# Row-wise cosine similarity: two rows per partition in three shared slots, products in place, all loads on the Sync queue

## Chip, cores and metric

One core of one Trainium2 chip (trn2). The metric is the device time of one execution in microseconds, the median of several runs. All times below are in microseconds unless ns is written.

## What is computed

```python
x, y: float32 [8192, 8192]
x_norm = np.linalg.norm(x, axis=1, keepdims=True)
y_norm = np.linalg.norm(y, axis=1, keepdims=True)
out = np.sum(x * y, axis=1) / (x_norm.squeeze() * y_norm.squeeze() + 1e-8)
```

For each of 8192 rows three sums over 8192 columns are needed: x·x, y·y and x·y. Each input is 268 MB and is read once; the output is 32 KB.

## The kernel before, in words

The 8192 rows are cut into 64 tiles of 128 rows, one row of 32 KB per partition. `xpool` and `ypool` have two buffers each, so two tiles of x and two of y fit. `issue_dma(t)` loads x of tile t from the Sync queue (SP, L63) and y of tile t from ScalarE's queue (ACT, L64), 4 MB each. The last tile is loaded in pieces: x in two halves (L59), y in pieces of 2048, 2048, 2048, 1024 and 1024 columns (L61).

`compute_tile(t)` gives VectorE (DVE) one fused multiply-and-sum over the tile (L96, which reads x and y, writes the products as bf16 into `prod_s` that nobody reads, and puts the sum into a column of `xy_acc`) and ScalarE two squares with sums (L106 for x, L112 for y, with `sq_s` as unread output). After each tile the load of tile t + 2 into the same buffers is issued, when both engines are done with them.

When tile 61 has been given out, `chain` turns the sums of tiles 0 to 61 into results: a product `nn` on DVE (L120), a square root `den` on ACT (L124), a reciprocal and a product on DVE, a transpose on TensorE, a copy and a store. The rest, after tile 62, is the last tile, piece by piece: squares on ACT (L167, L173 for x; L180 for y), a first piece of x squared on DVE (L157), products on DVE (L186), folds of the pieces' sums (L196, L200, L204), and the same chain for the last two tiles (L208 to L223).

The order on each engine is set by a scheduler from the program's order; a buffer of a pool is handed to the next tile when its last user is done. On DVE `nn` (L120) stands behind the product of tile 62; on ACT `den` (L124) stands ahead of the square of x of tile 62.

Of the kernel before, what the change touches and what calls it, by code (L numbers as in the profile page):

```python
# [7 lines left out]


@with_exitstack  # L10
def kernel(
# [5 lines left out]
):  # L17
    nc = tc.nc
    P = nc.NUM_PARTITIONS

    n_rows, n_cols = x.shape
    assert n_rows % P == 0
    n_tiles = n_rows // P

    fp32 = mybir.dt.float32
    bf16 = mybir.dt.bfloat16

    xv = x.rearrange("(t p) k -> t p k", p=P)
    yv = y.rearrange("(t p) k -> t p k", p=P)

    xpool = ctx.enter_context(tc.tile_pool(name="xpool", bufs=2))
    ypool = ctx.enter_context(tc.tile_pool(name="ypool", bufs=2))
    sqpool = ctx.enter_context(tc.tile_pool(name="sqpool", bufs=1))
    prodpool = ctx.enter_context(tc.tile_pool(name="prodpool", bufs=1))
    accpool = ctx.enter_context(tc.tile_pool(name="accpool", bufs=1))
    finpool = ctx.enter_context(tc.tile_pool(name="finpool", bufs=1))
    psumpool = ctx.enter_context(tc.tile_pool(name="psum", bufs=1, space=bass.MemoryType.PSUM))

    xtiles = [
        xpool.tile([P, n_cols], fp32, tag="x", name=f"xt{t}")  # L40
        for t in range(n_tiles)
    ]
    ytiles = [
        ypool.tile([P, n_cols], fp32, tag="y", name=f"yt{t}")
        for t in range(n_tiles)
    ]

    last = n_tiles - 1

    HALF = n_cols // 2  # L50

    XCH = [(0, HALF), (HALF, n_cols)]
    Q = n_cols // 8
    YCH = [(0, 2 * Q), (2 * Q, 4 * Q), (4 * Q, 6 * Q), (6 * Q, 7 * Q), (7 * Q, n_cols)]

    def issue_dma(t):
        if t == last:
            for a, b in XCH:
                nc.sync.dma_start(out=xtiles[t][:, a:b], in_=xv[t, :, a:b])  # L59
            for a, b in YCH:  # L60
                nc.scalar.dma_start(out=ytiles[t][:, a:b], in_=yv[t, :, a:b])  # L61
        else:
            nc.sync.dma_start(out=xtiles[t], in_=xv[t])  # L63
            nc.scalar.dma_start(out=ytiles[t], in_=yv[t])  # L64

    issue_dma(0)
    issue_dma(1)

    dummy = finpool.tile([P, 1], fp32, tag="dummy")
    nc.scalar.memzero(dummy)  # L70
    nc.scalar.sqrt(out=dummy, in_=dummy)  # L71

    ident = finpool.tile([P, P], fp32, tag="ident")
    make_identity(nc, ident)

    xx_acc = accpool.tile([P, n_tiles], fp32, tag="xx")
    yy_acc = accpool.tile([P, n_tiles], fp32, tag="yy")
    xy_acc = accpool.tile([P, n_tiles], fp32, tag="xy")

    prod_s = prodpool.tile([P, n_cols], bf16, tag="prod")  # L80
    sq_s = sqpool.tile([P, n_cols], bf16, tag="sq")

    res = finpool.tile([P, n_tiles], fp32, tag="res")
    nn = finpool.tile([P, n_tiles], fp32, tag="nn")
    den = finpool.tile([P, n_tiles], fp32, tag="den")
    rcp = finpool.tile([P, n_tiles], fp32, tag="rcp")
    res_t_ps = psumpool.tile([n_tiles, P], fp32, tag="res_t_ps")
    res_t = finpool.tile([n_tiles, P], fp32, tag="res_t")
    res_t_ps_last = psumpool.tile([2, P], fp32, tag="res_t_ps_last")
    res_row_last = finpool.tile([2, P], fp32, tag="res_row_last")  # L90
    out_v = out.rearrange("(t p) -> t p", p=P)

    def compute_tile(t):
        xt = xtiles[t]
        yt = ytiles[t]
        nc.vector.tensor_tensor_reduce(  # L96
            out=prod_s,
            in0=xt,
            in1=yt,
            scale=1.0,  # L100
            scalar=0.0,
            op0=mybir.AluOpType.mult,
            op1=mybir.AluOpType.add,
            accum_out=xy_acc[:, t:t + 1],
        )
        nc.scalar.activation(  # L106
            out=sq_s,
            in_=xt,
            func=mybir.ActivationFunctionType.Square,
            accum_out=xx_acc[:, t:t + 1],  # L110
        )
        nc.scalar.activation(  # L112
            out=sq_s,
            in_=yt,
            func=mybir.ActivationFunctionType.Square,
            accum_out=yy_acc[:, t:t + 1],
        )

    def chain(cols, ps, sb, orows):
        nc.vector.tensor_tensor(  # L120
            out=nn[:, cols], in0=xx_acc[:, cols], in1=yy_acc[:, cols],
            op=mybir.AluOpType.mult,
        )
        nc.scalar.activation(  # L124
            out=den[:, cols], in_=nn[:, cols],
            func=mybir.ActivationFunctionType.Sqrt,
        )
        nc.vector.reciprocal(out=rcp[:, cols], in_=den[:, cols])  # L128
        nc.vector.tensor_tensor(  # L129
            out=res[:, cols], in0=xy_acc[:, cols], in1=rcp[:, cols],  # L130
            op=mybir.AluOpType.mult,
        )
        nc.tensor.transpose(out=ps, in_=res[:, cols], identity=ident)  # L133
        nc.vector.tensor_copy(out=sb, in_=ps)
        nc.sync.dma_start(out=out_v[orows, :], in_=sb)

    for t in range(n_tiles - 1):
        compute_tile(t)
        if t + 2 < n_tiles:
            issue_dma(t + 2)  # L140
        if t == n_tiles - 3:
            e = slice(0, last - 1)
            chain(e, res_t_ps[e, :], res_t[e, :], e)

    lcol = slice(last, last + 1)
    tcols = slice(last - 1, last + 1)
    xt = xtiles[last]
    yt = ytiles[last]
    SPL = 2048
    xxp = accpool.tile([P, 3], fp32, tag="xxp")  # L150
    nych = len(YCH)
    yyp = accpool.tile([P, nych], fp32, tag="yyp")
    xyp = accpool.tile([P, nych], fp32, tag="xyp")
    xx_fold_s = accpool.tile([P, 3], fp32, tag="xxfolds")
    yy_fold_s = accpool.tile([P, nych], fp32, tag="yyfolds")

    nc.vector.tensor_tensor_reduce(  # L157
        out=prod_s[:, 0:SPL],
        in0=xt[:, 0:SPL],
        in1=xt[:, 0:SPL],  # L160
        scale=1.0,
        scalar=0.0,
        op0=mybir.AluOpType.mult,
        op1=mybir.AluOpType.add,
        accum_out=xxp[:, 0:1],
    )
    nc.scalar.activation(  # L167
        out=sq_s[:, SPL:HALF],
        in_=xt[:, SPL:HALF],
        func=mybir.ActivationFunctionType.Square,  # L170
        accum_out=xxp[:, 1:2],
    )
    nc.scalar.activation(  # L173
        out=sq_s[:, HALF:],
        in_=xt[:, HALF:],
        func=mybir.ActivationFunctionType.Square,
        accum_out=xxp[:, 2:3],
    )
    for k, (a, b) in enumerate(YCH):
        nc.scalar.activation(  # L180
            out=sq_s[:, a:b],
            in_=yt[:, a:b],
            func=mybir.ActivationFunctionType.Square,
            accum_out=yyp[:, k:k + 1],
        )
        nc.vector.tensor_tensor_reduce(  # L186
            out=prod_s[:, a:b],
            in0=xt[:, a:b],
            in1=yt[:, a:b],
            scale=1.0,  # L190
            scalar=0.0,
            op0=mybir.AluOpType.mult,
            op1=mybir.AluOpType.add,
            accum_out=xyp[:, k:k + 1],
        )
    nc.scalar.activation(  # L196
        out=xx_fold_s, in_=xxp, func=mybir.ActivationFunctionType.Copy,
        accum_out=xx_acc[:, lcol],
    )
    nc.scalar.activation(  # L200
        out=yy_fold_s, in_=yyp, func=mybir.ActivationFunctionType.Copy,
        accum_out=yy_acc[:, lcol],
    )
    nc.vector.tensor_reduce(  # L204
        out=xy_acc[:, lcol], in_=xyp, axis=mybir.AxisListType.X,
        op=mybir.AluOpType.add,
    )
    nc.vector.tensor_tensor(  # L208
        out=nn[:, tcols], in0=xx_acc[:, tcols], in1=yy_acc[:, tcols],
        op=mybir.AluOpType.mult,  # L210
    )
    nc.scalar.activation(  # L212
        out=den[:, tcols], in_=nn[:, tcols],
        func=mybir.ActivationFunctionType.Sqrt,
    )
    nc.vector.reciprocal(out=rcp[:, tcols], in_=den[:, tcols])
    nc.vector.tensor_tensor(  # L217
        out=res[:, tcols], in0=xy_acc[:, tcols], in1=rcp[:, tcols],
        op=mybir.AluOpType.mult,
    )  # L220
    nc.tensor.transpose(out=res_t_ps_last[0:2, :], in_=res[:, tcols], identity=ident)  # L221
    nc.vector.tensor_copy(out=res_row_last[0:2, :], in_=res_t_ps_last[0:2, :])  # L222
    nc.sync.dma_start(out=out_v[last - 1:last + 1, :], in_=res_row_last[0:2, :])  # L223


# [1 line left out]
_INS = ['x', 'y']  # L227
_OUTS = [((8192,), 'float32')]
# [25 lines left out]
```

## Time and profile before

| | us |
|---|---|
| median of 3 runs (lowest, highest) | 1271.8 (1271.54, 1272.02) |
| the profiled execution | 1271.54 |
| its span, first to last instruction | 1269.8 |
| busy: DVE / ACT | 561.2 / 914.4 |
| L96 product, 128x8192, one | 8.693 |
| L106 and L112 square, 128x8192, one | 7.030 |
| L186 product, 128x2048 / 128x1024 | 2.292 / 1.189 |
| L180 square, 128x2048 / 128x1024 | 1.892 / 1.038 |
| load of 4 MB, issue to landing, median: x (Sync) / y (ACT) | 29.6 / 24.9 |
| DMA packets of 32768 B | 16128 of 19227 |

The DMA share is the mean busy share of the core's 16 DMA engines; a load of 128 partitions is spread over all 16, eight partitions to each. "Landing" is the time at which the last of the 16 has reported. An engine's idle time is put down to what released it.

### The profile page before, as it was taken

What the parts mean: (1) busy time and instruction counts of PE and PEld (TensorE: products, weight loads), DVE (VectorE), ACT (ScalarE), POOL (GpSimd) and SP (SyncE); (2) the same over time, 40 slices, a digit from 0 to 9 for tenths busy, and PEclk for the clock granted to TensorE, in tenths of its full rate; (3) what the DMA queues carried; (4) which work ended last, traced back from release to release, by engine and by line L of the source; (5) the groups of instructions that cost most, each with busy time, mean ns of one, the idle gap of its engine ahead of it and who ended that gap; (6) DMA issues with size and microseconds to landing.
All of it is one profiled execution on the core that took longest, in us unless ns stands there. A gap on an engine that the chain in (4) does not pass through costs nothing.

```text
span 1269.8 us, 874 instructions
## 1 busy us (share of the span) xinstructions
PE 0.8 (0%) x2; PEld 0.2 (0%) x2; DVE 561.2 (44%) x147; ACT 914.4 (72%) x276; POOL 0.7 (0%) x6
## 2 busy tenths in 40 slices
PE   0000000000000000000000000000000000000000
PEld 0000000000000000000000000000000000000000
DVE  2354354453453543534534435445345354353454
ACT  3786686776776867767768668677686686776748
POOL 0000000000000000000000000000000000000000
DMA  9999999999999999999999999999999999999992
GB/s 412 430 429 429 429 433 434 437 430 430 429 429 433 434 433 434 430 429 429 434 434 431 434 431 429 429 435 433 431 431 433 429 431 435 430 433 431 433 424 110
DMA packets 19227, 536.97 MB, mean 423 GB/s; under 512 B 2132, under 2 KB 2196, under 8 KB 2452
## 3 DMA queue, kind: packets, MB, share of 16 engines
q10 hardware_dynamic: 9792, 268.44, 49.2%
q1 hardware_dynamic: 9428, 268.47, 49.2%
q14 instruction: 7, 0.06, 0.0%
HBM read 536.87 MB, written 0.03 MB: 423 GB/s over the span
## 4 chain that ended last, share of the span: by engine, by line
DMA 68%; issue 15%; DVE 11%; ACT 5%; DVEq 0%; PE 0%; SPq 0%
DMA xt<-in_x_dram 36%; DMA yt<-in_y_dram 32%; DVE prod_s L96 11%; ACT sq_s L112 3%; ACT sq_s L106 2%; ACT sq_s L180 1%; ACT L71 0%; DVEq L96 0%; PE res_t_ps_last L221 0%; DVE xy_acc L96 0%; SPq L63 0%; DVE res_row_last L222 0%; ACT sq_s L173 0%; ACT sq_s L167 0%; ACT den L212 0%
## 5 line engine op out<-in xcount | busy, mean ns | idle before, releaser
L96 DVE CUSTOM_DVE_ANT_0 prod_s<-xt,yt 128x8192 bf16<-128x8192 f32 x63 | 547.6, 8693 | 689.7 <-DMA yt<-in_y_dram 656.2
L106 ACT ACTIVATE sq_s<-xt 128x8192 bf16<-128x8192 f32 x63 | 442.9, 7030 | 334.0 <-DMA xt<-in_x_dram 334.0
L112 ACT ACTIVATE sq_s<-yt 128x8192 bf16<-128x8192 f32 x63 | 442.9, 7030 | 1.9
L106 ACT ACTIVATION_READ_ACCUMULATOR sq_s<-xt 128x1 f32 x63 | 11.8, 187 | 0.0
L112 ACT ACTIVATION_READ_ACCUMULATOR sq_s<-yt 128x1 f32 x63 | 11.7, 186 | 0.0
L124 ACT ACTIVATE den<-nn 128x62 f32<-128x62 f32 x1 | 0.3, 255 | 14.3 <-DVE nn L120 14.3
L186 DVE CUSTOM_DVE_ANT_0 prod_s<-xt,yt 128x2048 bf16<-128x2048 f32 (+1 forms) x5 | 9.3, 1851 | 2.1 <-DMA yt<-in_y_dram 2.0
L180 ACT ACTIVATE sq_s<-yt 128x2048 bf16<-128x2048 f32 (+1 forms) x5 | 7.8, 1551 | 0.0
L208 DVE TENSOR_TENSOR nn<-xx_acc,yy_acc 128x2 f32<-128x2 f32 x1 | 0.2, 162 | 14.0 <-ACT yy_fold_s L200 14.0
L96 DVE DVE_READ_ACCUMULATOR2_ANT xy_acc<- 128x1 f32 x63 | 5.2, 83 | 0.0
L173 ACT ACTIVATE sq_s<-xt 128x4096 bf16<-128x4096 f32 x1 | 3.6, 3599 | 0.0
L70 ACT ACT_TABLE_LOAD x1 | 1.3, 1283 | 1.6 <-PEq L238 1.6
L157 DVE CUSTOM_DVE_ANT_0 prod_s<-xt 128x2048 bf16<-128x2048 f32 x1 | 2.3, 2286 | 0.0
L167 ACT ACTIVATE sq_s<-xt 128x2048 bf16<-128x2048 f32 x1 | 1.9, 1909 | 0.0
L71 ACT ACT_TABLE_LOAD x1 | 1.3, 1283 | 0.0
L133 PE MATMUL res_t_ps<-ident,res 128*62 128x128 f32 x1 | 0.4, 393 | 1251.0 <-DVE res L129 1251.0
L180 ACT ACTIVATION_READ_ACCUMULATOR sq_s<-yt 128x1 f32 x5 | 0.9, 186 | 0.0
L128 DVE RECIPROCAL rcp<-den 128x62 f32<-128x62 f32 x1 | 0.5, 535 | 0.0
L222 DVE COPY res_row_last<-res_t_ps_last 2x128 f32<-2x128 f32 x1 | 0.3, 279 | 0.5 <-PE res_t_ps_last L221 0.5
L186 DVE DVE_READ_ACCUMULATOR2_ANT xyp<- 128x1 f32 x5 | 0.4, 82 | 0.0
L221 PE MATMUL res_t_ps_last<-ident,res 128*2 128x128 f32 x1 | 0.4, 373 | 15.7 <-DVE res L217 15.7
L212 ACT ACTIVATE den<-nn 128x2 f32<-128x2 f32 x1 | 0.2, 203 | 0.2 <-DVE nn L208 0.2
(23 smaller groups left out, 3.9 us busy)
## 6 DMA issues: line engine op xcount, KB each, us to landing
yt<-in_y_dram ACTq DMA_DIRECT2D x63, 4096.0 KB, 24.9
xt<-in_x_dram SPq DMA_DIRECT2D x63, 4096.0 KB, 29.6
xt<-in_x_dram SPq DMA_DIRECT2D x2, 2048.0 KB, 25.4
yt<-in_y_dram ACTq DMA_DIRECT2D x3, 1024.0 KB, 20.4
yt<-in_y_dram ACTq DMA_DIRECT2D x2, 512.0 KB, 21.7
out_dram<-res_t SPq DMA_DIRECT2D x1, 31.0 KB
out_dram<-res_row_last SPq DMA_DIRECT2D x1, 1.0 KB
```

Source lines behind the costliest of these rows:

```text
L70: nc.scalar.memzero(dummy)
L71: nc.scalar.sqrt(out=dummy, in_=dummy)
L96: nc.vector.tensor_tensor_reduce(out=prod_s, in0=xt, in1=yt, scale=1.0, scalar=0.0, op0=mybir.AluOpType.mult, op1=mybir.AluOpType.add, acc ...
L106: nc.scalar.activation(out=sq_s, in_=xt, func=mybir.ActivationFunctionType.Square, accum_out=xx_acc[:, t:t + 1],)
L112: nc.scalar.activation(out=sq_s, in_=yt, func=mybir.ActivationFunctionType.Square, accum_out=yy_acc[:, t:t + 1],)
L128: nc.vector.reciprocal(out=rcp[:, cols], in_=den[:, cols])
L133: nc.tensor.transpose(out=ps, in_=res[:, cols], identity=ident)
L157: nc.vector.tensor_tensor_reduce(out=prod_s[:, 0:SPL], in0=xt[:, 0:SPL], in1=xt[:, 0:SPL], scale=1.0, scalar=0.0, op0=mybir.AluOpType.mult ...
L167: nc.scalar.activation(out=sq_s[:, SPL:HALF], in_=xt[:, SPL:HALF], func=mybir.ActivationFunctionType.Square, accum_out=xxp[:, 1:2],)
L173: nc.scalar.activation(out=sq_s[:, HALF:], in_=xt[:, HALF:], func=mybir.ActivationFunctionType.Square, accum_out=xxp[:, 2:3],)
L180: nc.scalar.activation(out=sq_s[:, a:b], in_=yt[:, a:b], func=mybir.ActivationFunctionType.Square, accum_out=yyp[:, k:k + 1],)
L186: nc.vector.tensor_tensor_reduce(out=prod_s[:, a:b], in0=xt[:, a:b], in1=yt[:, a:b], scale=1.0, scalar=0.0, op0=mybir.AluOpType.mult, op1= ...
```

## The change

The first 62 tiles' rows become 31 groups of 256 rows. In a group partition p holds rows 2p and 2p + 1, which lie side by side in memory, as one run of 64 KB; one load brings 8 MB of x or of y. One pool of three slots of 64 KB per partition (`slots`) serves x and y in turn, so the slots go x0, y0, x1, then y1 into the slot of x0, x2 into the slot of y0, and so on. All loads are issued from the Sync queue, in the order in which they are used.

Per group ACT squares the two rows of x and of y (output: one byte per element into `junk`). DVE copies the last 896 columns of x into `side`, multiplies the first rows (8192 columns), then the second rows without the last 896 columns (7296), both written over x in float32, and then `side` by the end of y, starting from the sum so far. After the second product nothing reads x's slot any more. The last two tiles of 128 rows (62 and 63) take one slot each: tile 62 as two loads of 32 KB per partition, tile 63 in the same pieces as before. `finish` takes the place of `chain`; it adds 1e-8 to the product of the norms, and its results of a group are transposed for even and odd rows apart. The first piece of the last x is squared on ACT, not on DVE.

```diff
-    xpool = ctx.enter_context(tc.tile_pool(name="xpool", bufs=2))
-    ypool = ctx.enter_context(tc.tile_pool(name="ypool", bufs=2))
...
+    G = n_rows // (2 * P) - 1
+    SIDE = 896
+    xg = x[0:G * 2 * P, :].rearrange("(g p j) k -> g p (j k)", p=P, j=2)
+    yg = y[0:G * 2 * P, :].rearrange("(g p j) k -> g p (j k)", p=P, j=2)
...
+    slots = ctx.enter_context(tc.tile_pool(name="slots", bufs=3))
+    sidepool = ctx.enter_context(tc.tile_pool(name="side", bufs=1))
...
+    def slot(name):
+        return slots.tile([P, 2 * K], FP32, tag="slot", name=name)
...
-            nc.sync.dma_start(out=xtiles[t], in_=xv[t])
-            nc.scalar.dma_start(out=ytiles[t], in_=yv[t])
+    def load(g):
+        xs[g] = slot(f"xg{g}")
+        nc.sync.dma_start(out=xs[g], in_=xg[g])
+        ys[g] = slot(f"yg{g}")
+        nc.sync.dma_start(out=ys[g], in_=yg[g])
...
+    junk = sidepool.tile([P, K], U8, tag="junk")
+    side = sidepool.tile([P, SIDE], FP32, tag="side")
...
+    def square(src, acc):
+        nc.scalar.activation(
+            out=junk[:, 0:src.shape[-1]], in_=src, func=ACTF.Square,
+            accum_out=acc)
+    def dot(a, b, acc, init=0.0):
+        nc.vector.tensor_tensor_reduce(
+            out=a, in0=a, in1=b, scale=1.0,
+            scalar=init, op0=ALU.mult, op1=ALU.add, accum_out=acc)
+    for g in range(G):
+        xt, yt = xs.pop(g), ys.pop(g)
+        c = 2 * g
+        square(xt[:, 0:K], xx[:, c:c + 1])
+        square(xt[:, K:], xx[:, c + 1:c + 2])
+        nc.vector.tensor_copy(out=side, in_=xt[:, 2 * K - SIDE:])
+        dot(xt[:, 0:K], yt[:, 0:K], xy[:, c:c + 1])
+        dot(xt[:, K:2 * K - SIDE], yt[:, K:2 * K - SIDE], xyh[:, c + 1:c + 2])
+        square(yt[:, 0:K], yy[:, c:c + 1])
+        square(yt[:, K:], yy[:, c + 1:c + 2])
+        dot(side, yt[:, 2 * K - SIDE:], xy[:, c + 1:c + 2], init=xyh[:, c + 1:c + 2])
+        if g + 1 < G:
+            load(g + 1)
...
+    def finish(cols):
+        nc.vector.tensor_mul(out=den[:, cols], in0=xx[:, cols], in1=yy[:, cols])
+        nc.scalar.activation(out=den[:, cols], in_=den[:, cols], func=ACTF.Sqrt)
+        nc.vector.tensor_scalar_add(out=den[:, cols], in0=den[:, cols], scalar1=EPS)
         nc.vector.reciprocal(out=rcp[:, cols], in_=den[:, cols])
+        nc.vector.tensor_mul(out=res[:, cols], in0=xy[:, cols], in1=rcp[:, cols])
...
+    s0 = slot("tail0")
+    s1 = slot("tail1")
+    nc.sync.dma_start(out=s0[:, 0:K], in_=xv[nt - 2])
+    nc.sync.dma_start(out=s0[:, K:], in_=yv[nt - 2])
...
+    for a, b in XCH:
+        nc.sync.dma_start(out=s1[:, a:b], in_=xv[nt - 1, :, a:b])
+    for a, b in YCH:
+        nc.sync.dma_start(out=s1[:, K + a:K + b], in_=yv[nt - 1, :, a:b])
+    gcols = slice(0, 2 * G)
+    finish(gcols)
...
+    c = nt - 2
+    square(s0[:, 0:K], xx[:, c:c + 1])
+    square(s0[:, K:], yy[:, c:c + 1])
+    dot(s0[:, 0:K], s0[:, K:], xy[:, c:c + 1])
...
+    square(s1[:, 0:H], xxp[:, 0:1])
+    square(s1[:, H:K], xxp[:, 1:2])
     for k, (a, b) in enumerate(YCH):
+        square(s1[:, K + a:K + b], yyp[:, k:k + 1])
+        dot(s1[:, a:b], s1[:, K + a:K + b], xyp[:, k:k + 1])
...
+    tcols = slice(nt - 2, nt)
+    finish(tcols)
```

More of the change, by code (lines that the diff above doesn't have):

```diff
@@ L7 @@
 from concourse._compat import with_exitstack
+FP32 = mybir.dt.float32
+U8 = mybir.dt.uint8
+ALU = mybir.AluOpType
+ACTF = mybir.ActivationFunctionType
+EPS = 1e-8
 @with_exitstack
@@ L19 @@
     P = nc.NUM_PARTITIONS
[L21 to L26, printed above, removed]
+    n_rows, K = x.shape
+    G = n_rows // (2 * P) - 1
+    SIDE = 896
+    xg = x[0:G * 2 * P, :].rearrange("(g p j) k -> g p (j k)", p=P, j=2)
+    yg = y[0:G * 2 * P, :].rearrange("(g p j) k -> g p (j k)", p=P, j=2)
     xv = x.rearrange("(t p) k -> t p k", p=P)
     yv = y.rearrange("(t p) k -> t p k", p=P)
-    xpool = ctx.enter_context(tc.tile_pool(name="xpool", bufs=2))
@@ L32 @@
-    ypool = ctx.enter_context(tc.tile_pool(name="ypool", bufs=2))
[L33 to L62, printed above, removed]
-            nc.sync.dma_start(out=xtiles[t], in_=xv[t])
-            nc.scalar.dma_start(out=ytiles[t], in_=yv[t])
@@ L66 @@
-    issue_dma(0)
-    issue_dma(1)
-    dummy = finpool.tile([P, 1], fp32, tag="dummy")
+    nt = n_rows // P
+    slots = ctx.enter_context(tc.tile_pool(name="slots", bufs=3))
+    sidepool = ctx.enter_context(tc.tile_pool(name="side", bufs=1))
+    small = ctx.enter_context(tc.tile_pool(name="small", bufs=1))
+    psumpool = ctx.enter_context(
+        tc.tile_pool(name="psum", bufs=1, space=bass.MemoryType.PSUM))
+    def slot(name):
+        return slots.tile([P, 2 * K], FP32, tag="slot", name=name)
@@ new lines @@
+    xs, ys = {}, {}
+    def load(g):
[3 more added lines that the diff above has]
+        nc.sync.dma_start(out=ys[g], in_=yg[g])
+    load(0)
+    xx = small.tile([P, nt], FP32, tag="xx")
+    yy = small.tile([P, nt], FP32, tag="yy")
+    xy = small.tile([P, nt], FP32, tag="xy")
+    xyh = small.tile([P, nt], FP32, tag="xyh")
+    den = small.tile([P, nt], FP32, tag="den")
+    rcp = small.tile([P, nt], FP32, tag="rcp")
+    res = small.tile([P, nt], FP32, tag="res")
@@ L70 @@
+    ident = small.tile([P, P], FP32, tag="ident")
+    dummy = small.tile([P, 1], FP32, tag="dummy")
+    junk = sidepool.tile([P, K], U8, tag="junk")
+    side = sidepool.tile([P, SIDE], FP32, tag="side")
     nc.scalar.memzero(dummy)
     nc.scalar.sqrt(out=dummy, in_=dummy)
-    ident = finpool.tile([P, P], fp32, tag="ident")
     make_identity(nc, ident)
-    xx_acc = accpool.tile([P, n_tiles], fp32, tag="xx")
-    yy_acc = accpool.tile([P, n_tiles], fp32, tag="yy")
-    xy_acc = accpool.tile([P, n_tiles], fp32, tag="xy")
@@ L80 @@
[L80 to L127, printed above, removed]
-        nc.vector.reciprocal(out=rcp[:, cols], in_=den[:, cols])
[L129 to L178, printed above, removed]
-    for k, (a, b) in enumerate(YCH):
[L180 to L203, printed above, removed]
-    nc.vector.tensor_reduce(
[L205 to L222, printed above, removed]
@@ L223 @@
-    nc.sync.dma_start(out=out_v[last - 1:last + 1, :], in_=res_row_last[0:2, :])
+    def square(src, acc):
[3 more added lines that the diff above has]
+    def dot(a, b, acc, init=0.0):
+        nc.vector.tensor_tensor_reduce(
+            out=a, in0=a, in1=b, scale=1.0,
[13 more added lines that the diff above has]
+            load(g + 1)
@@ new lines @@
+    nc.sync.dma_start(out=s0[:, K:], in_=yv[nt - 2])
+    H = K // 2
+    Q = K // 8
+    XCH = [(0, H), (H, K)]
+    YCH = [(0, 2 * Q), (2 * Q, 4 * Q), (4 * Q, 6 * Q), (6 * Q, 7 * Q), (7 * Q, K)]
+    for a, b in XCH:
[4 more added lines that the diff above has]
+    finish(gcols)
+    orow = small.tile([G, P, 2], FP32, tag="orow")
+    for j in range(2):
+        ps = psumpool.tile([G, P], FP32, tag=f"ps{j}", name=f"ps{j}")
+        nc.tensor.transpose(out=ps, in_=res[:, j:2 * G:2], identity=ident)
+        nc.vector.tensor_copy(out=orow[:, :, j], in_=ps)
@@ new lines @@
+    nc.sync.dma_start(
+        out=out[0:G * 2 * P].rearrange("(g q) -> g q", q=2 * P),
+        in_=orow.rearrange("g p j -> g (p j)"))
+    c = nt - 2
+    square(s0[:, 0:K], xx[:, c:c + 1])
+    square(s0[:, K:], yy[:, c:c + 1])
+    dot(s0[:, 0:K], s0[:, K:], xy[:, c:c + 1])
+    c = nt - 1
+    xxp = small.tile([P, 2], FP32, tag="xxp")
+    yyp = small.tile([P, len(YCH)], FP32, tag="yyp")
+    xyp = small.tile([P, len(YCH)], FP32, tag="xyp")
+    fold = small.tile([P, len(YCH)], FP32, tag="fold")
@@ new lines @@
+    square(s1[:, 0:H], xxp[:, 0:1])
+    square(s1[:, H:K], xxp[:, 1:2])
+    for k, (a, b) in enumerate(YCH):
+        square(s1[:, K + a:K + b], yyp[:, k:k + 1])
+        dot(s1[:, a:b], s1[:, K + a:K + b], xyp[:, k:k + 1])
+    nc.scalar.activation(out=fold[:, 0:2], in_=xxp, func=ACTF.Copy, accum_out=xx[:, c:c + 1])
+    nc.scalar.activation(out=fold, in_=yyp, func=ACTF.Copy, accum_out=yy[:, c:c + 1])
+    nc.vector.tensor_reduce(
+        out=xy[:, c:c + 1], in_=xyp, axis=mybir.AxisListType.X, op=ALU.add)
@@ L227 @@
+    tcols = slice(nt - 2, nt)
+    finish(tcols)
+    psl = psumpool.tile([2, P], FP32, tag="psl")
+    orl = small.tile([2, P], FP32, tag="orl")
+    nc.tensor.transpose(out=psl, in_=res[:, tcols], identity=ident)
+    nc.vector.tensor_copy(out=orl, in_=psl)
+    nc.sync.dma_start(out=out.rearrange("(t p) -> t p", p=P)[nt - 2:nt, :], in_=orl)
 _INS = ['x', 'y']
```

## The prediction

> **What bounds the kernel now.** I read the page, then the table by stage, the waits, the timeline of a middle tile and of the last 30 us, and last the trace's packet records (start, duration, size and queue of each DMA packet). Page: busy time by engine, and two rows of the 40 slices.
>
> ```profile
> PE 0.8 (0%) x2; PEld 0.2 (0%) x2; DVE 561.2 (44%) x147; ACT 914.4 (72%) x276; POOL 0.7 (0%) x6
> DMA  9999999999999999999999999999999999999992
> GB/s 412 430 429 429 429 433 434 437 430 430 429 429 433 434 433 434 430 429 429 434 434 431 434 431 429 429 435 433 431 431 433 429 431 435 430 433 431 433 424 110
> ```
>
> No compute engine is full; the DMA engines are, until the last slice. Stage table (window, length, busy time and count of PE, PEld, DVE, ACT, POOL, then clock, DMA share, GB/s):
>
> ```profile
> 120.00:600.00 480.00, 0.00 (x0) 0.00 (x0) 217.50 (x50) 354.62 (x99) 0.00 (x0) 1.00 1.00 432
> 1229.00:1250.00 21.00, 0.00 (x0) 0.00 (x0) 18.80 (x13) 11.97 (x4) 0.00 (x0) 1.00 0.84 348
> 1250.00:1270.00 20.00, 0.77 (x2) 0.21 (x2) 2.99 (x11) 16.35 (x21) 0.00 (x0) 1.00 0.01 2
> ```
>
> Up to 1249 us the transfers set the time; in the last 20 us nothing is loaded and ACT works. Waits (who, for whom: total us, times, longest):
>
> ```profile
> DVE prod_s L96 <- DMA yt<-in_y_dram: 656.2, 61, 11.7
> ACT sq_s L106 <- DMA xt<-in_x_dram: 334.0, 62, 19.6
> ...
> ACT den L124 <- DVE nn L120: 14.3, 1, 14.3
> ```
>
> Both engines wait for data in every tile: compute time counts only where it delays a transfer. The third row is the exception; it shows again in the timeline (start, us, engine, line, what, idle before):
>
> ```profile
> 1229.13 8.69 DVE L96 CUSTOM_DVE_ANT_0 prod_s<-xt,yt 128x8192 bf16<-128x8192 f32 x1 [10.66 <-DMA yt<-in_y_dram]
> ...
> 1237.74 0.22 DVE L120 TENSOR_TENSOR nn<-xx_acc,yy_acc 128x62 f32<-128x62 f32 x1
> ...
> 1238.00 0.26 ACT L124 ACTIVATE den<-nn 128x62 f32<-128x62 f32 x1 [14.35 <-DVE nn L120]
> 1238.16 7.01 ACT L106 ACTIVATE sq_s<-xt 128x8192 bf16<-128x8192 f32 x1
> ...
> 1265.99 0.19 ACT L200 ACTIVATION_READ_ACCUMULATOR yy_fold_s<-yyp 128x1 f32 x1
> ```
>
> x of tile 62 is there at 1228.3 (last packet), but ACT's queue holds the early `den` in front of its square; `den` waits for `nn`, which on DVE stands behind the product of tile 62. ACT starts at 1238.16 and never idles again until 1266.18, while the last load packet ends at 1248.83. So the span is 1.78 us before the first packet, 1247.05 of loading, 17.35 of ACT backlog, and 3.6 from the last fold to the end (1269.8). The profiled execution took 1271.54, its span and 1.74 around it; the median of the runs is 0.26 above it.
>
> **The change, part by part.** *Packets.* From 100 us on, a packet of 32768 B follows the one before it on its DMA engine after 1213.8 ns on average; one of 8192 B mostly after 306, one of 4096 B after 155. From the last two a byte costs 0.0369 ns, which leaves 4 ns of the small packets and 6 of the large one that do not grow with size; I take 5. Each DMA engine moves 992 such packets in the 31 groups; if each pair becomes one packet of 65536 B, 496 x 5 ns = 2.5 us go. Bounds: in the first 40 us the spacing was 1209.4 for all, so at best 992 x 4.4 ns + 2.5 = 6.9 us go; the slow tail of the rows is 1221, so at worst 992 x 7 ns = 7 us come. 60 fewer loads, each ending in a 6 ns semaphore packet on each engine: -0.4.
>
> A rule against it: the Trainium skill, "DMA: Bandwidth & Descriptors", section "Latency and other measured facts", has copies slow down when the rows of a tile lie a large power of two apart, 207 GB/s instead of 214 at 512 KiB. As an estimate from that page 3% of the group loads would be about +40 us. No run here shows that pitch: rows of a group lie 64 KiB apart, and the nearest row is the present 32 KiB at 432 GB/s.
>
> *The new wait.* Three slots for x and y mean that y of group g+1 goes into the slot of x of group g. Its issue on the Sync queue waits for the second product of the group (the order of instructions confirms this one, not the product on `side`); behind it in that queue stands only x of g+2, which has 19 us more. Count from the last packet of y of g. In the old trace the product starts 0.65 us after the last packet of y (63 tiles, 0.63 to 0.8, once 1.07). The product of 8192 takes 8.69 and the next starts 0.04 later; the slope of 1.042 ns per column between the rows of 2048 (2.29) and 8192 makes 7.76 for 7296; from its end to the issue on Sync it is 0.08 (62.65 to 71.42 with one product). So the issue comes at 0.65 + 8.73 + 7.76 + 0.08 = 17.22. From an issue to packets only the start of the kernel shows idle engines: issue at 0.73, first packets at 1.78 to 2.06 (one at 2.63), which took 1.6 to 2.0 instead of 1.21; that is as if they had begun 1.54 to 2.04 after the issue. So y of g+1 can flow at 18.76 to 19.26. Meanwhile x of g+1, issued long before, keeps each engine busy for 8 packets of about 2.42 = 19.37. Room: 0.1 to 0.6 us, no stall on the slowest DMA engine; faster engines may run dry without cost. I put 0.05 us x 31 = 1.5 us for odd events (five late packets of 0.35 to 0.65 us are in the old trace). The bound on the other side: products that write f32 over their input are in no row (bf16 elsewhere); were they 4% slower, 0.66 us, a stall of up to 0.5 us per group would follow.
>
> The same page, section "Anatomy of one DMA", puts most of a fixed 2.0 us (measured on GpSimd's path) behind the last byte. Taken for the 0.65, the estimate is a stall of 0.7 to 1.2 us per group, 23 to 38 us, and a slower kernel. The 63 rows here say 0.65, and the row decides.
>
> *Hidden at no cost.* `side` is copied while DVE waits for y (656 us of such waits; without that cover 1.2 us x 31, the price of a 1024-column product). The squares write bytes instead of bf16: ACT needs 28.6 of 38.8 us per group, so even 30% more would be covered there. The product in place needs the square of that x done: x is squared 19 us before y lands. The new y queue: ACT no longer issues (0.33 us each, idle time). Loads begin as before; x lands alone at about 21 us and y at 41, but all three slots are filled by then.
>
> *The end.* Let E be the last load packet. Behind y of the last group, the single queue brings x and y of tile 62 (9.71 each), x of 63 (9.79) and its five y pieces (9.82): that y lands at E - 39.08. ACT starts 0.5 after it and then has, from the start-to-start times of the old end: two y squares 14.30; x and y of 62 14.30; `den` 0.16 (its `nn` is ready at about E - 22, ACT comes to it at E - 17); two halves of 4096 at 3.60; three of 2048 at 1.89; two of 1024 at 1.04; folds 0.19 and 0.28. Sum 44.2, so ACT is done at E + 5.6 and never waits for data. DVE: tile 62's product is behind `finish` and done at about E - 5.9; the pieces (2.33 and 1.2 each, each waiting for its square of x) end at E + 3.7, 1.9 before ACT. What was 17.35 of backlog is 5.6: -11.75. `nn` no longer holds up ACT; late next is ACT's plain load of work. The chain behind it is as before (3.6) and one small add longer (`reciprocal` of that size 0.17): +0.2.
>
> **Sum.** E = 1248.83 - 2.5 - 0.4 + 1.5 = 1247.4. Span = 1247.4 + 5.6 + 3.8 = 1256.8; with 1.74, 1258.5; against the median of 1271.8 that is **1258.8 us**, 13.0 faster (1.0%).
>
> **Rivals.** *A stall in each group (slower).* The place is the issue of y of g+1 on Sync behind the second product; the price is 31 times what 17.22 + start-up exceeds 19.37. It decides from 13.0/31 = 0.42 us per group, which needs about 0.5 to 1.0 us that my rows do not show: products 3 to 6% slower in f32, or start-up of 2.6 to 3.0 with engines busy. At 0.7 us: 1280.5. For it: the room is the difference of two numbers near 19, and the single old row of a start-up is of an idle queue. Against it: DVE's time per column did not move with DMA traffic (8.691 to 8.694 in all 63).
> *A small stall* of 0.1 to 0.42 us: 1261 to 1271, the tail's gain mostly given back to the groups.
> *Packets no better or worse.* If a run of 64 KB still goes as two packets, or if one stream read by all engines is slower than x and y alternating: 1261.3 with no gain, 1268.3 at 1221 ns per 32 KB; beyond that no row.
>
> **How the numbers follow.** Forecast 0.62, its own range 1252.5 (best packets, no stall: 1258.8 - 4.4 - 1.5) to 1264. Small stall 0.10 (0.07 faster, 0.03 within 0.2%). Packets 0.08 (0.05 faster, 0.01 the same, 0.02 slower). Large stall 0.20, slower. That makes 0.74 faster, 0.04 within 0.2% (2.5 us, about what a measurement of this kernel can tell), 0.22 slower. The range of 8 in 10 begins at 1252 and must take in small stalls, slow packets and a third of the large ones, up to 0.55 us per group (1276).
>
> **What would show it.** Right: packets of 65536 B about 2.42 us apart; the second product to the Sync issue and that issue to its first packets such that DMA share stays 1.00 and GB/s about 433 in the groups; ACT without idle time from the last group's y on, done 5 to 6 us after the last load. Wrong: DMA share of 0.97 or less in the group stages with idle gaps between x of g+1 and y of g+1 (the stall); products over 8.8 us; packets over 2.44 us; or ACT still more than 10 us behind at the end.

## The result, and the profile after

The changed kernel takes 1286.2 us (median of 4 runs, 1283.66 to 1288.25), the kernel before 1271.8. The ratio is 1.011, with a 95% interval of 1.009 to 1.013: slower by about 14 us, where 1258.8 was forecast and 1276 was the end of the range. The profiled execution took 1283.66, the fastest of the four, with a span of 1281.5, and what follows is read from it.

Page of the kernel after: DMA share and GB/s in 40 slices of the span, then the chain that ended last, by engine.

```profile
DMA  9999999999999999999999999999999999999996
GB/s 425 421 425 430 419 407 444 430 395 444 407 423 425 428 425 419 413 421 415 425 425 425 425 422 422 401 426 425 425 450 415 407 428 428 423 423 421 428 420 275
...
DMA 57%; DVE 38%; ACT 2%; issue 2%; DVEq 0%; SPq 0%; PE 0%; ACTq 0%
```

The last slice has become better (275 GB/s where there were 110), and most of the others worse: 395 to 450, mostly about 425, where the kernel before mostly held 429 to 435. The digit 9 in every slice hides that: it means 90% or more. The chain now runs through VectorE for 38% of the span, although VectorE is busy for less than half of it. The chain itself, by time, in the middle of the run (start, us, what):

```profile
559.13 8.69 DVE xg L82
...
567.83 7.67 DVE xg L82
...
575.54 24.20 DMA yg<-in_y_dram
...
599.87 8.69 DVE xg L82
```

That is a loop of its own: product, product, issue of the next y, its landing, product. The waits name the same loop from both sides, first VectorE (who, for whom: total us, times, longest), then the Sync queue's own:

```profile
DVE xg L82 <- DMA yg<-in_y_dram: 608.0, 31, 21.0
```

```profile
SPq L55 <- DVE xyh L82: 1101.5, 30, 38.0
```

The first is no news, since VectorE waited for y before, too. The second is: the load of y (L55) waits in the Sync queue for the sum of the second product (`xyh`) in all 30 groups in which a slot has to come free. Timeline of two groups (start, us, engine, line, what, idle before):

```profile
559.13 8.69 DVE L82 CUSTOM_DVE_ANT_0 xg<-xg,yg 128x8192 f32<-128x8192 f32 x1 [20.64 <-DMA yg<-in_y_dram]
...
567.75 7.75 DVE L82 CUSTOM_DVE_ANT_0 xg<-xg,yg 128x7296 f32<-128x7296 f32 x1
...
575.54 0.33 SPq L55 DMA_DIRECT2D yg<-in_y_dram  x1
...
599.87 8.69 DVE L82 CUSTOM_DVE_ANT_0 xg<-xg,yg 128x8192 f32<-128x8192 f32 x1 [20.80 <-DMA yg<-in_y_dram]
...
616.28 0.33 SPq L55 DMA_DIRECT2D yg<-in_y_dram  x1
...
638.62 8.69 DVE L82 CUSTOM_DVE_ANT_0 xg<-xg,yg 128x8192 f32<-128x8192 f32 x1 [18.77 <-DMA yg<-in_y_dram]
```

The products are as fast as ever, 8.69 and 7.75. From product to product one group takes 40.74, the next 38.75; sixteen packets of 64 KB in a row, at their median of 2.418, make 38.69. So some groups are at the floor and others 2 us above it. Two numbers from the trace's packet records set the scene: y is issued 16.89 us after the last packet of the y before (16.86 to 17.03), and after that issue the last of the 16 DMA engines has 2.50 us of x left (2.32 to 3.05). I call these 2.50 the **room**: the time that a newly issued load has to get going before the queue behind it is empty.

The packet records also say what happens in that room. For each group: when the DMA engines ended x, when they began y, both counted from the issue of y, and the loss, which is how much later the last engine ended its first packet of y than the end of x and 2.42. The records name no engine; packets are put to engines by the end of one and the start of the next, and each load's last packet on an engine by the 4-byte packet that follows it:

```
issue of y   x ends (first, median, last)   y begins (median, last)   loss
375.66       1.47  1.79  2.46               1.80  3.87                1.78
575.54       0.22  0.77  2.43               1.27  3.29                2.11
616.28      -0.30 -0.06  2.52               1.14  2.51                0.00
655.02       1.58  1.74  2.59               1.74  2.59                0.00
733.48       0.92  1.43  2.58               2.32  3.36                2.16
774.44       0.11  0.61  2.44               1.19  3.77                2.26
```

In 15 of the 30 groups the loss is 0.85 to 2.3 us, together 24.7; in the other 15 it is at most 0.5, together 1.3. An engine that had been idle for a while begins y 0.95 to 1.5 after the issue, with a first packet of up to 3.5 us, and mostly costs nothing (616.28: 13 of 16 were dry at the issue). An engine that still had work when y was issued sometimes goes on without a gap (655.02), and sometimes begins y late: in the 15 groups with a loss the latest begins 2.8 to 3.9 us after the issue (733.48, 774.44). At 375.66 it is the engine that had most work left: it ends x at 2.46 and then stands idle until 3.87, while the other 15 began y within 2.0. The slowest of the 16 decides when y has landed.

The end of the kernel (timeline):

```profile
1254.15 0.24 ACT L102 ACTIVATE den<-den 128x62 f32<-128x62 f32 x1
1254.30 7.01 ACT L76 ACTIVATE junk<-tail 128x8192 uint8<-128x8192 f32 x1
...
1277.54 0.18 ACT L149 ACTIVATION_READ_ACCUMULATOR fold<-yyp 128x1 f32 x1
```

`den` no longer makes ACT wait, and ACT's last fold ends at 1277.72. The last load packet ends at 1272.98, so that ACT's backlog is 4.74, where it was 17.35, and 3.83 follow. Against the kernel before, the end of loading came 24.15 later and what follows it is 12.4 shorter: 11.7 more in the span.

### The profile page after: what moved, and what is told of

The parts are those of the page before. It is cut to its first block, busy times and chain, and to the rows that moved or that the text cites. A ratio compares the mean times of both kernels' runs of the same rounds, so it can differ in the third digit from the quotient of the medians.

```text
span 1281.5 us, 845 instructions
## 1 busy us (share of the span) xinstructions
PE 1.0 (0%) x3; PEld 0.3 (0%) x3; DVE 583.6 (46%) x241; ACT 916.8 (72%) x276; POOL 0.7 (0%) x6
## 4 chain that ended last, share of the span: by engine, by line
DMA 57%; DVE 38%; ACT 2%; issue 2%; DVEq 0%; SPq 0%; PE 0%; ACTq 0%
DMA yg<-in_y_dram 57%; DVE xg L82 38%; ACT junk L76 2%; DVEq L82 0%; DVE xyh L82 0%; SPq L53 0%; PE psl L156 0%; ACT den L102 0%; ACT fold L149 0%; DVE orl L157 0%; DVE xy L82 0%; DVE den L103 0%; DVE rcp L104 0%; DVE den L101 0%; DVE res L105 0%
## 5 line engine op out<-in xcount | busy, mean ns | idle before, releaser
L82 DVE CUSTOM_DVE_ANT_0 xg<-xg,yg 128x8192 f32<-128x8192 f32 (+1 forms) x62 | 507.5, 8223 | 608.0 <-DMA yg<-in_y_dram 608.0
L76 ACT ACTIVATE junk<-yg 128x8192 uint8<-128x8192 f32 x62 | 435.9, 7030 | 185.2 <-DMA yg<-in_y_dram 184.3
L76 ACT ACTIVATE junk<-xg 128x8192 uint8<-128x8192 f32 x62 | 435.9, 7030 | 174.9 <-DMA xg<-in_x_dram 173.9
L91 DVE COPY side<-xg 128x896 f32<-128x896 f32 x31 | 19.4, 627 | 78.1 <-DMA xg<-in_x_dram 78.1
L82 DVE CUSTOM_DVE_ANT_0 side<-side,yg,xyh 128x896 f32<-128x896 f32 x31 | 35.7, 1152 | 1.1
L76 ACT ACTIVATE junk<-tail 128x2048 uint8<-128x2048 f32 (+3 forms) x9 | 29.1, 3234 | 0.2
L82 DVE CUSTOM_DVE_ANT_0 tail<-tail 128x2048 f32<-128x2048 f32 (+2 forms) x6 | 17.8, 2998 | 1.1 <-DMA tail<-in_y_dram 1.1
L76 ACT ACTIVATION_READ_ACCUMULATOR junk<-yg 128x1 f32 x62 | 11.6, 186 | 0.0
L76 ACT ACTIVATION_READ_ACCUMULATOR junk<-xg 128x1 f32 x62 | 11.6, 186 | 0.0
L82 DVE DVE_READ_ACCUMULATOR2_ANT xy<- 128x1 f32 x63 | 5.2, 83 | 0.0
L127 PE MATMUL ps<-ident,res 128*31 128x128 f32 x2 | 0.6, 407 | 1255.6 <-DVE res L105 1255.6
L127 PEld LDWEIGHTS ps<-ident,res 128*31 128x31 f32 x2 | 0.2, 138 | 1255.6 <-issue 1255.6
```

Of the source, the lines that this page charges most:

```text
L76: nc.scalar.activation(out=junk[:, 0:src.shape[-1]], in_=src, func=ACTF.Square, accum_out=acc)
L82: nc.vector.tensor_tensor_reduce(out=a, in0=a, in1=b, scale=1.0, scalar=init, op0=ALU.mult, op1=ALU.add, accum_out=acc)
L91: nc.vector.tensor_copy(out=side, in_=xt[:, 2 * K - SIDE:])
L127: nc.tensor.transpose(out=ps, in_=res[:, j:2 * G:2], identity=ident)
```

## The experiments

My theory after this result: the load of y has too little room, and busy DMA engines take up a load late. The rivals were 64 KB packets or their order in memory, a collision with the load of the next x, issued 1.2 us behind it, and later that the number of loads decides and not the room. All edits are to the changed kernel, but for the tail alone. In each session the kernel before ran too, at 1271.6 to 1271.7.

**Less room.** The second product is made longer, so that x's slot comes free 0.46 later.

```diff
-    SIDE = 896
+    SIDE = 448
```

> SIDE 448 instead of 896: the second product is 448 columns (0.47 us) longer, nothing else moves. Theory A (late release: the Sync issue of the next y comes 16.9 us after the last y packet, x of the next group lasts 19.3, and descriptors reach busy DMA engines up to 4.4 us after an issue): 0.47 us more stall in most of the 31 groups, about +14 us, 1300. Theory B (packets of 64 KB are what starts late): also slower, as the room is the same quantity for it. Theory C (one queue and one stream are slower in themselves, whatever the release): no change, 1286.

Measured: 1297.5 (1296.9 to 1299.3), ratio 1.021 (1.019 to 1.022), room 2.03. A group takes 40.16 instead of 39.69 in the profiled runs, and the medians are 11.3 apart, 0.38 per group: half a microsecond of room less costs nearly as much in every group. The 4.4 us in the expectation are too long; packet by packet, the latest start in the changed kernel is 3.87 us after the issue.

**32 KB packets.** The rows p and p + 128 share a partition, so that each is a run of its own; y is changed likewise, and the results are written in that order.

```diff
-    xg = x[0:G * 2 * P, :].rearrange("(g p j) k -> g p (j k)", p=P, j=2)
+    xg = x[0:G * 2 * P, :].rearrange("(g j p) k -> g p j k", p=P, j=2)
...
-        nc.sync.dma_start(out=xs[g], in_=xg[g])
+        nc.sync.dma_start(out=xs[g].rearrange("p (j k) -> p j k", j=2), in_=xg[g])
```

> A partition holds rows p and p + 128 of a group instead of two adjacent rows, so each load is two runs of 32 KB per partition; slots, queue, waits and products stay. Theory A: the release is as late as before, 1280 to 1292. Theory B: late descriptors wait behind shorter packets, most of the 30 us of stalls goes, 1257 to 1268. Theory C: as A.

Measured: 1297.0 (1293.3 to 1298.4), ratio 1.019 (1.018 to 1.021), 40.16 per group at a room of 2.46. The 64 KB packets are not what slows the kernel: without them it is slower still, by more than packets alone explain (see below). Why the stall is larger here at the same room is open.

**y in two loads.** The first product can start on the first half.

```diff
-        nc.sync.dma_start(out=ys[g], in_=yg[g])
+        nc.sync.dma_start(out=ys[g][:, 0:K], in_=yg[g, :, 0:K])
+        nc.sync.dma_start(out=ys[g][:, K:], in_=yg[g, :, K:])
```

> y of a group is loaded as two loads, first rows then second rows (runs of 32 KB); x stays one run of 64 KB. The first product then runs while the second half of y lands, and the slot of x comes free 8.4 us after the last y packet instead of 16.9. Theory A: no stalls, loads end near 1247, 1256 to 1261. Theory B: the same or a few us more. Theory C: no change, 1284 or more.

Measured: 1255.8 (1255.6 to 1256.1), ratio 0.9875 (0.986 to 0.989). Stage table and timeline of this kernel:

```profile
120.00:600.00 480.00, 0.00 (x0) 0.00 (x0) 227.67 (x88) 350.69 (x100) 0.00 (x0) 1.00 1.00 433
```

```profile
614.90 8.69 DVE L83 CUSTOM_DVE_ANT_0 xg<-xg,yg 128x8192 f32<-128x8192 f32 x1 [9.12 <-DMA yg<-in_y_dram]
...
624.62 7.76 DVE L83 CUSTOM_DVE_ANT_0 xg<-xg,yg 128x7296 f32<-128x7296 f32 x1 [1.02 <-DMA yg<-in_y_dram]
...
632.41 0.33 SPq L55 DMA_DIRECT2D yg<-in_y_dram  x1
```

The second product alone is left behind the end of y: the issue comes 8.4 after it instead of 16.9, the room is 10.96, the DMA share is 1.00 at 433 GB/s, and a group takes 38.84. The same stage of the changed kernel:

```profile
120.00:600.00 480.00, 0.00 (x0) 0.00 (x0) 218.13 (x85) 342.08 (x97) 0.00 (x0) 1.00 0.99 422
```

A loss of over 2% of the traffic shows as 0.99 of DMA share: of the 27.7 us that each DMA engine loses on average, 13.1 lie in first packets that last longer, and these count as busy. The GB/s tell it better.

**The tail alone.** In the kernel before, `chain` is given out one tile later.

```diff
-        if t == n_tiles - 3:
+        if t == n_tiles - 2:
```

> The kernel before, with the early chain given out one tile later, so that ACT squares x of tile 62 before it waits for the product of norms. If the 17.35 us of backlog at its end come from that wait: ACT starts 7.1 us of work earlier, 1264.7. If ACT's backlog has another cause: 1271.8.

Measured: 1264.5 (1264.5 to 1264.9), ratio 0.994 (0.993 to 0.996), 7.1 less than before. Its waits and its timeline at the place that the prediction showed:

```profile
ACT den L124 <- DVE nn L120: 1.7, 1, 1.7
```

```profile
1229.28 7.03 ACT L106 ACTIVATE sq_s<-xt 128x8192 bf16<-128x8192 f32 x1 [5.53 <-DMA xt<-in_x_dram]
...
1238.09 0.26 ACT L124 ACTIVATE den<-nn 128x62 f32<-128x62 f32 x1 [1.69 <-DVE nn L120]
```

The wait of 14.3 is 1.7, and ACT begins the square of tile 62 at 1229.28 instead of 1238.16. What the prediction read from the tail holds.

**A little more room.** Here x's last 1792 columns go aside, in bf16 to fit the memory.

```diff
-    SIDE = 896
+    SIDE = 1792
...
-    side = sidepool.tile([P, SIDE], FP32, tag="side")
+    side = sidepool.tile([P, SIDE], mybir.dt.bfloat16, tag="side")
```

> SIDE 1792 instead of 896, the copy in bf16 so that it takes no more memory: the second product is 896 columns (0.93 us) shorter, so the slot of x comes free 0.93 us earlier; the copy is rounded to bf16, which touches 1792 of 16384 products per pair of rows. Theory A: with 448 columns the groups took 40.16 us, with 896 39.69, the same 0.47 apart as the products, and without stalls 38.84; so 38.84 to 39.0 here, 1259 to 1266. If the late start of single DMA engines were the same size whatever the room: 1286.

Measured: 1277.8 (1276.2 to 1280.5), ratio 1.004 (1.003 to 1.006), room 3.38. It moved the right way, by 8.4, and missed what was expected by over 10: room of 3.4 is not enough. The latest of 16 engines comes later than I had allowed for.

**y in two loads, 32 KB packets.** The edits of the second and third experiment together.

> As with y in two loads, but a partition holds rows p and p + 128, so x too goes in runs of 32 KB: every packet of the groups is 32 KB and nothing stalls. If a packet costs about 5 to 7 ns beyond its bytes (prediction; 2422 against 2 x 1218 ns in the trace with both sizes): 248 packets fewer per DMA engine are lost, +1.2 to +3.5 us against 1255.8, so 1257 to 1259.3. If the 11 us between 64 and 32 KB packets of the earlier pair were a matter of packets alone and not of the stalls: 1261 or more.

Measured: 1258.1 (1258.0 to 1258.1), ratio 0.989 (0.988 to 0.991), room 11.0. With enough room the packet size of x costs 2.3 us, as expected.

**y from ACT's queue.** A single run.

```diff
-        nc.sync.dma_start(out=ys[g], in_=yg[g])
+        nc.scalar.dma_start(out=ys[g], in_=yg[g])
```

> The changed kernel with y loaded from ScalarE's queue, x from Sync, three slots and waits as they are. If only the release of x's slot matters (theory A alone): 1280 to 1290. If the order within one queue matters, because x of g+2 then shares the DMA engines with y of g+1, both land together after 39 us and nothing is queued while the two products run: about 57 us per group, near 1800.

Measured: 1750.5, the DMA share 0.73 in the groups. Timeline of this kernel:

```profile
600.07 8.69 DVE L82 CUSTOM_DVE_ANT_0 xg<-xg,yg 128x8192 f32<-128x8192 f32 x1 [36.94 <-DMA yg<-in_y_dram]
...
616.49 0.33 ACTq L55 DMA_DIRECT2D yg<-in_y_dram  x1
...
617.72 0.33 SPq L53 DMA_DIRECT2D xg<-in_x_dram  x1
```

On one queue y of the next group goes ahead of x of the group after it. On two queues the two flow side by side, and y, which is needed first, lands when both are nearly done (last packets of y at 654.8, of x at 657.2): VectorE waits 36.94 instead of about 20. With three slots, one queue is part of the change and no detail.

**Everything together.** y in two loads; no copy aside (the second product takes all 8192 columns, since there is room); VectorE squares 1792 columns of the last x, which takes work from ACT's backlog.

```diff
-        nc.vector.tensor_copy(out=side, in_=xt[:, 2 * K - SIDE:])
...
-        dot(xt[:, K:2 * K - SIDE], yt[:, K:2 * K - SIDE], xyh[:, c + 1:c + 2])
+        dot(xt[:, K:], yt[:, K:], xy[:, c + 1:c + 2])
...
-        dot(side, yt[:, 2 * K - SIDE:], xy[:, c + 1:c + 2], init=xyh[:, c + 1:c + 2])
...
+    D = 2 * SIDE
+    nc.vector.tensor_tensor_reduce(
+        out=side, in0=s1[:, 0:D], in1=s1[:, 0:D], scale=1.0,
+        scalar=0.0, op0=ALU.mult, op1=ALU.add, accum_out=xxp[:, 2:3])
+    square(s1[:, D:H], xxp[:, 0:1])
```

> y in two loads, no copy aside (the second product takes all 8192 columns; the slot comes free about 9.4 us after the last y packet, still 10 us ahead of need), and DVE squares 1792 of the first 4096 columns of the last x. Groups as in the run with y in halves (38.84); ACT's backlog after the last load 1.6 us shorter: 1254.3. If the copy aside still mattered: 1260 or more.

Measured: 1254.6 (1254.5 to 1254.8), ratio 0.987 (0.985 to 0.988), room 10.0: the fastest full version, 17 us under the kernel before. Against y in two loads alone (span 1254.1, now 1252.8) loading ends 1.0 earlier and the rest is 0.3 shorter; the two were run in different sessions and the intervals of their ratios overlap, so that I don't divide this step further.

**The next issue moved away.** The product on `side` is held back until the next x has landed, so that the issue of x (L53) follows that of y by 4.9 us instead of 1.2. Its timeline:

```profile
609.75 0.33 SPq L55 DMA_DIRECT2D yg<-in_y_dram  x1
614.67 0.33 SPq L53 DMA_DIRECT2D xg<-in_x_dram  x1
```

```diff
+        if g:
+            cp = 2 * g - 1
+            nc.vector.tensor_scalar(
+                out=gate[:, cp:cp + 1], in0=xt[:, 0:1], scalar1=0.0,
+                scalar2=xyh[:, cp:cp + 1], op0=ALU.mult, op1=ALU.add)
+            side_dot(g - 1, gate)
```

> The changed kernel, but the product on side (in two bf16 buffers) is held until x of the next group has landed, so x of g+2 is issued some 4 us after y of g+1 has its packets going, not 1.2 us after its issue. The release of y of g+1 stays where it was. Theory D (the descriptors of y come late to single DMA engines because the next issue on the same queue follows 1.2 us later): stalls go, 1257 to 1265. Theory A2 (a busy DMA engine takes up a new load late whatever else is issued): 1280 to 1290.

Measured: 1284.2 (1279.1 to 1286.2), ratio 1.010 (1.009 to 1.012), at a room of 2.54. Nothing is gained that the spread of these runs would show: the late starts do not come from the next issue.

**Room of 4.7 us.** y in two loads of 2304 and 14080 columns, the first product in two pieces.

```diff
+        nc.sync.dma_start(out=ys[g][:, 0:C0], in_=yg[g, :, 0:C0])
+        nc.sync.dma_start(out=ys[g][:, C0:], in_=yg[g, :, C0:])
...
-        dot(xt[:, 0:K], yt[:, 0:K], xy[:, c:c + 1])
+        dot(xt[:, 0:C0], yt[:, 0:C0], xyh[:, c:c + 1])
+        dot(xt[:, C0:K], yt[:, C0:K], xy[:, c:c + 1], init=xyh[:, c:c + 1])
```

> y of a group in two loads, 2304 and 14080 columns; the product of the first piece runs before the rest has landed, so the slot of x comes free 2.3 us earlier and about 4.7 us remain from the issue to the end of x (2.4 in the changed kernel, 3.4 with 1792 columns aside, 10.9 with y in halves). Theory A2 with late starts of up to 6 us on one of 16 engines: most of the stall goes but not all, 39.0 to 39.3 per group, 1260 to 1270. If the late start grew with the room: 1275 or more.

Measured: 1259.0 (1258.7 to 1259.5), ratio 0.990 (0.989 to 0.992), 38.89 per group at a room of 4.68. All but the stall's last traces are gone, a little better than expected.

**Two loads at the same room, and one load with room.** So far every kernel without a stall had y in two loads. These two runs take the pair apart. First two loads whose second is 128 columns, which give hardly any room:

```diff
+        nc.sync.dma_start(out=ys[g][:, 0:2 * K - 128], in_=yg[g, :, 0:2 * K - 128])
+        nc.sync.dma_start(out=ys[g][:, 2 * K - 128:], in_=yg[g, :, 2 * K - 128:])
```

> Two kernels with more room have so far run without a stall, and both load y in two pieces; here y comes in two loads (16256 columns, then the last 128, which only the product on side reads) while the room grows by only about 0.15 us (128 of 16384 columns of a y that takes 19.4). Theory that the room decides: about as the changed kernel, 1280 to 1290 (128 small packets per group add at most 3). Rival, that splitting the load itself cures the late starts (a second issue wakes the engines): 1255 to 1260, DMA share 1.00 in the groups.

Then one load, with the second product cut short, so that 2560 columns of every odd row's x*y are left out:

```diff
-        dot(xt[:, K:2 * K - SIDE], yt[:, K:2 * K - SIDE], xyh[:, c + 1:c + 2])
+        dot(xt[:, K:K + 4736], yt[:, K:K + 4736], xyh[:, c + 1:c + 2])
```

> y in one load as in the changed kernel; the second product stops after 4736 columns (the next 2560 columns of each odd row's x*y are left out), so that the slot of x is released 2560 x 1.042 ns = 2.7 us earlier and the room is about 5.1 us. Theory that the room decides: no stall, 1255 to 1261, as the kernel with 4.7 us (1259.0). Rival, that splitting the load is what cures: a small gain over the kernel with 3.4 us (1277.8), 1268 to 1277.

Measured: two loads at a room of 2.65 take 1294.2 (1292.9 to 1296.3), ratio 1.018 (1.016 to 1.020); one load at a room of 5.01 takes 1255.7 (1255.5 to 1255.9), ratio 0.987 (0.986 to 0.989). The stage table of the first:

```profile
120.00:600.00 480.00, 0.00 (x0) 0.00 (x0) 218.00 (x84) 341.89 (x96) 0.00 (x0) 1.00 0.98 418
```

Timeline and stage table of the latter:

```profile
584.83 8.69 DVE L82 CUSTOM_DVE_ANT_0 xg<-xg,yg 128x8192 f32<-128x8192 f32 x1 [18.77 <-DMA yg<-in_y_dram]
593.44 5.08 DVE L82 CUSTOM_DVE_ANT_0 xg<-xg,yg 128x4736 f32<-128x4736 f32 x1
598.57 0.33 SPq L55 DMA_DIRECT2D yg<-in_y_dram  x1
...
623.55 8.69 DVE L82 CUSTOM_DVE_ANT_0 xg<-xg,yg 128x8192 f32<-128x8192 f32 x1 [18.79 <-DMA yg<-in_y_dram]
```

```profile
120.00:600.00 480.00, 0.00 (x0) 0.00 (x0) 200.31 (x90) 355.52 (x100) 0.00 (x0) 1.00 1.00 433
```

The load, its packets and its queue are those of the changed kernel; only its issue comes 2.55 earlier, and 30 us are gone. VectorE works less in this run, but that is not the cure: at a room of 4.68 and 10.96 it did all its work, and the stall was gone there too. Splitting cures nothing by itself; room does. The first of the pair is 4 us above what was expected and 8 above the changed kernel at nearly the same room, as with 32 KB packets: more pieces seem to make the stall larger, and I did not find out why.

The rooms and times together, y in one load with 64 KB packets unless noted:

| room, us | us per group | median, us |
|---|---|---|
| 2.03 | 40.16 | 1297.5 |
| 2.50 (the change) | 39.69 | 1286.2 |
| 3.38 | 39.59 | 1277.8 |
| 4.68 (two loads) | 38.89 | 1259.0 |
| 5.01 | 38.76 | 1255.7 |
| 10.96 (two loads) | 38.84 | 1255.8 |

The middle column is from the profiled runs, of which that at 3.38 was the slowest of its four and that of the change the fastest.

## Why the prediction was wrong

**The new wait: wrong, and it decided.** The place was right, the issue of y behind the second product, and so was the time up to it: 17.22 worked out, 16.89 measured. The room left after it was 2.5, more than the start-up of 1.54 to 2.04 that I set against it. What failed is that start-up: it came from the only row of the old trace, idle engines at the start of the kernel, and I took it for engines with work. Idle engines about kept to it (0.95 to 1.5 after the issue, and the first packet up to 1.1 longer), and "faster engines may run dry without cost" held too (616.28). But of 16 engines with work left, the latest began as late as 3.9 us after the issue, in effect 4.7 with a longer first packet counted in. So 1.5 us of allowance (0.05 per group) became about 26. It is the rival of a stall in each group, by the second of the two conditions given there (a slower start with engines busy), with about 0.85 per group in the place of 0.7; it had a chance of 0.20, too little for a room whose margin was 0.1 to 0.6 by my own sum.

In the sum: the last load ended at 1272.98 instead of 1247.4. Of these 25.6, the 30 groups after the first bring 0.80 each (39.69 instead of 38.89), 24.0 (38.89 is the predicted end of the last group's y, 1247.4 - 39.08, less the 41.67 of the first, by 30), and the way from the last group's y to the last load 1.5 (40.59 instead of 39.08; the prediction's own four terms add up to 39.03). That is mostly the same stall once more: x of tile 63 is issued when 2.48 of work is left. The run with a room of 5.0 ended loading at 1243.65, so without the stall the sum would have erred the other way.

**Packets: right in kind, undersized as far as the runs tell.** They are single packets of 65536 B, 2.418 long in the median, 2.42 predicted. The gain was put at 2.5 with 6.9 as the best; between the kernel of 32 KB packets with y in two loads (loading ends at 1249.10) and that of 64 KB packets with a room of 5.0 (1243.65) it is 5.4, of which the packets of x alone make 2.2 (loading ends at 1246.88 where y still comes in halves of 32 KB). That comparison also has 31 loads fewer and DVE's shorter product in it, so that the rest of the 5.4 is not shown to be packets alone.

**Products in float32, copy aside, byte squares: right.** 8.69, 7.75 and 7.03 are the old rates; the bound of 4% was not needed. All of it lies in waits.

**The end: right, with some luck in the number.** `den` holds nothing up, ACT has no idle time from the last group's y to its last fold, and 3.83 follow (3.8 predicted). But ACT took 45.3 from that y on, where the sum has 44.7, and its backlog is 4.74 instead of 5.6 only because the loads behind that y were 1.5 late. With a room of 5.0 they took 39.21, and the backlog was 6.25. The tail alone gives 7.1 in the old kernel, and the whole 12.4 here.

**The rules weighed.** The Trainium skill, "DMA: Bandwidth & Descriptors", section "Anatomy of one DMA", puts most of a fixed 2.0 us (measured on GpSimd's path) behind the last byte. The prediction's estimate from it, 23 to 38 us, was near the 26 that came. The trace does not show it there: from the last packet of y to the product it is 0.45 to 0.62 us now. The loss sits between the issue and the first packets, so the number met by chance. The same page's slowdown for rows that lie a large power of two apart is stated from 512 KiB on, and no run here has that pitch; at the 64 KiB of this change it is 433 GB/s wherever there is room.

**What stays open.** Why a DMA engine with work left takes up the next load as late as 3.9 us after its issue, in about half of the groups; that the issue of the next x is not the cause is shown. And why smaller or more packets make it worse at the same room.

## What to carry to other kernels

When buffers come free late, count for each transfer how much work the DMA engines still have when it is issued, and do not set a mean or an idle start against it: the last of 16 engines decides, and here it took about 5 us of queued work before the stall was gone. A slot can be freed earlier at little cost (y in halves ended loading 3.2 us later than one load with room, 1246.88 against 1243.65) by cutting the load that its last reader waits for, so that most of the compute lies under the transfer. A margin that is the difference of two numbers near 19 deserves a chance near one half, not one in five.

## What the runs showed of the hardware

- A load issued to a queue that still had 2.5 us of work began on single DMA engines 2.8 to 3.9 us after the issue, in half of the groups; on idle ones 0.95 to 1.5 after it. The first packet then lasted up to 3.8 instead of 2.42.
- A kernel with this stall spreads over 4.6 us between runs (1283.7 to 1288.3); the four with a room of 5 or more spread over 0.1 to 0.5.
- A fused product that writes float32 over its own input takes the same 8.69 us as one that writes bf16 elsewhere, and a square that writes bytes the same 7.03.
- Between 120 and 600 us a DMA share of 0.98 to 0.99 went with 418 to 426 GB/s, one of 1.00 with 432 to 433. Between 600 and 1200 us the kernel with a room of 3.38 shows 1.00 at 424: the share can hide the stall altogether.
